# Modulation products of a two-block network: four blocks of k on the four column tiles of the array in one visit

## The chip, the cores and the metric

The kernel runs on one core of a Trainium2 chip. Times are microseconds (us) of device time of one execution; the time before is the median of three runs.

## The reference, cut to what matters

The network has a first block of two layers and a second block. Each layer of the first block scales and shifts its input and gates its output by vectors that are products of a condition vector with a large matrix, once for the latent rows (`c`) and once for the context rows (`c_ctx`):

```python
sc, scc = jax.nn.silu(c), jax.nn.silu(c_ctx)          # [1, 2048], [2048]
for l in range(DEPTH):                                 # two layers
    shift_l, scale_l, gate_l = jnp.split((sc @ mod_w[l] + mod_b[l])[:, None, :], 3, axis=-1)
    shift_c, scale_c, gate_c = jnp.split(scc @ mod_w[l] + mod_b[l], 3, axis=-1)
    hl = xl * (1.0 + scale_l) + shift_l                # 256 latent rows
    hc = xc * (1.0 + scale_c) + shift_c                # 256 context rows
    ...                                                # layer 0: a recurrence; layer 1: attention
    xl = layer_norm(DEEPNORM_ALPHA * xl + gate_l * yl, ln_g[l], ln_b[l])
    xc = layer_norm(DEEPNORM_ALPHA * xc + gate_c * yc, ln_g[l], ln_b[l])
```

`mod_w` is [2, 2048, 6144] in float32, 100 MB. Layer 0 is a mixer with a linear recurrence over 256 context and 256 latent tokens, in both directions, for 16 heads of 64; its input projection is 2048 x 6400. The second block has a cross attention to 256 memory rows, whose keys and values are products with `w_xkv`.

## The kernel before

The products with the modulation matrix have only two rows (`c` and `c_ctx`), so the condition is the stationary operand: for each block k of 128 rows of the matrix, `SC` holds a column pair, and a product takes 32 columns from there, of which the first two count. The moving operand is 128 x 512 elements of the matrix in float32. Thirty-two columns are one of four column tiles of the array, and the block k goes to tile `k % 4`, which writes partitions 32q to 32q + 31 of one accumulator; the four partial sums are added afterwards, by a product with `sel`. A column block of 512 outputs needs 16 blocks k.

`mod` (L332) is a generator that emits these products. It loads tiles of 128 x 2 x 512 (two blocks k, 512 KB) through SP's queue. Each step, a visit, takes one tile: two products on two column tiles (L354), tiles 0 and 1 or tiles 2 and 3. Eight visits make a column block; then ACT copies the accumulator (L359), and a ninth step turns or adds the partial sums (L364, L374). There are 24 column blocks in all: 8 of layer 0 in the head, the other 16 (layer 0's gate, all of layer 1) as fillers of layer 0's recurrence.

The order of PE is the order in which the Python code emits; a scheduler of the library orders DVE, SP and the other queues (and ACT after the first part of the head).

- The head (`head`, L1559): first the memory's rows are turned (L961) with one visit in each of eight steps; then the memory's keys (L1527 to L1529, weights split into a high part by ACT, L187, and a low part by DVE, L188) run with five visits to eight steps of six products, and with the filters (L1654, L1663) between. The tiles of `mod_w` go to a ring of eight buffers ("A"), seven loads ahead.
- The recurrence (`l0_body`, L802): 16 units, each cut into steps that wait on ACT and DVE (L685, L746, L751, L757, L763, L764). Between two steps `fill` emits products of `filler` for a number of us that follows from the work left and the steps left. `filler` yields groups of three products of the input projection (L468, L469, L470; 8 groups use up one weight chunk of 512 KB) and, of every 44 groups, takes a step of `mod` after each fourth until nine are done. `mod` yields an assumed 0.3 us for a visit and 0.9 us for the ninth step. Here the tiles of `mod_w` and the weight chunks share the buffers `raw`, four in all; `mod` loads one tile ahead.

Of the kernel before, what the change touches and what calls it, by code (L numbers as in the profile page):

```python
# [21 lines left out]
P = 128  # L22
# [27 lines left out]
def _consts():  # L50
    f = np.float32
    out = {}
# [40 lines left out]
    # real DFT of length 512, packed: rows 0..255 Re(0..255), row 256 Re(256), rows 257.. Im(1..255)  # L93
# [43 lines left out]
class _K:  # L137
# [12 lines left out]
    def big(s, tag):  # L150
        """sixteen [P, 2, 256] tiles (high and low part), in pairs"""
        out = _L()
        out.pairs = [s.T("%s%d" % (tag, j), [P, 2, 2, 256], F32R) for j in range(8)]
        out += [pr[:, i] for pr in out.pairs for i in range(2)]
        return out

    def big0(s, tag):
        """sixteen [P, 512] tiles, in pairs"""
        out = _L()
        out.pairs = [s.T("%s%d" % (tag, j), [P, 2, 512], F32R) for j in range(8)]  # L160
        out += [pr[:, i] for pr in out.pairs for i in range(2)]
        return out
# [5 lines left out]
    # ---------------------------------------------------------------- weights  # L168
# [32 lines left out]
    def formB(s, W, c0, toks, accs, nk=KT, sub=2):  # L201
        """toks: list of functions k -> (hi, lo) stationary APs"""
        nc = s.nc
        for kc in range(nk // sub):
            hi, lo = s.wload(W[kc * sub * P:(kc + 1) * sub * P, c0:c0 + 512].rearrange("(k p) c -> p k c", p=P), sub, 512)
            for kk in range(sub):
                k = kc * sub + kk
                for tk, acc in zip(toks, accs):
                    xh, xl = tk(k)
                    nc.tensor.matmul(acc, xh, hi[:, kk], start=k == 0, stop=False)  # L210
                    nc.tensor.matmul(acc, xh, lo[:, kk], start=False, stop=False)
                    nc.tensor.matmul(acc, xl, hi[:, kk], start=False, stop=k == nk - 1)
                yield

    # ---------------------------------------------------------------- setup
    def setup(s):
# [25 lines left out]
        # parameter vectors, feature-major  # L242
# [51 lines left out]
    def params(s, g):  # L294
        nc = s.nc
        ps = s.PS("sc")
        nc.tensor.transpose(ps[:, 0:128], s.prow[g], s.ident)
        nc.vector.tensor_copy(s.PT[:, g], ps[:, 0:128])
        if g != 1:
            return  # L300
        # 1 - mu, halves used by the tanh forms of the sigmoids
        s.PM = s.T("PM", [P, 128])
        nc.vector.tensor_scalar(s.PM, s.PT[:, 1], -1.0, 1.0, MUL, ADD)
        s.PH = s.T("PH", [P, 128])
        nc.vector.tensor_scalar(s.PH, s.PT[:, 1], 0.5, None, MUL)
        s.PHM = s.T("PHM", [P, 128])
        nc.vector.tensor_scalar(s.PHM, s.PT[:, 1], -0.5, 1.0, MUL, ADD)
# [7 lines left out]
    # ---------------------------------------------------------------- modulation  # L315
    def mod_prep(s):
# [8 lines left out]
        # column pairs (c, c_ctx) per k; each product takes 32 columns, of which the first two count  # L325
# [6 lines left out]
    def mod(s, l, j0, j1, ahead=1, ring=None):  # L332
        """columns of 512 of the modulation of layer l; yields the time of the products it has emitted"""
# [11 lines left out]
        for i, (j, kc) in enumerate(lst):  # L345
            for q in range(ahead + 1):
                load(i + q)
            raw = got.pop(i)
            if kc == 0:
                acc = s.PS("acc" if ring is None else "iv")  # L350
            for kk in range(2):
                k = kc * 2 + kk
                q = k % 4
                nc.tensor.matmul(acc[32 * q:32 * q + 32], s.SC[:, 2 * k:2 * k + 32], raw[:, kk], start=k < 4, stop=k >= 12, tile_position=(0, 32 * q))  # L354
            if kc < 7:
                yield 0.3
                continue
            rows = s.T("sg", [P, 512])
            nc.scalar.copy(rows, acc)  # L359
            yield 0.3  # L360
# [18 lines left out]
    # ---------------------------------------------------------------- layer 0  # L379
    def l0_rows(s):  # L380
        """token rows of the context and of x, as lists of 128-wide pieces"""
# [18 lines left out]
    def l0_h(s, toks):  # L400
        nc = s.nc
        s.AH, s.AL = s.big0("A"), s.big0("B")
        for k in range(16):
# [4 lines left out]
            md = s.MOD[0]  # lat: tokens 256:512, ctx: 0:256  # L408
# [21 lines left out]
    def l0_lora(s):  # L430
        nc, W = s.nc, s.I["ev_w_in"][0]
        # per direction: high part on the first 64 partitions, low part on the others
# [15 lines left out]
    def stream(s, srcs, ahead=1):  # L448
        """weight chunks (source, k, c) split ahead of their use: call with an index"""
# [12 lines left out]
    def atoms(s, i, hX, lX, acc):  # L462
        """formA as a generator that yields the time of the products it has emitted"""
# [38 lines left out]
    def cat_out(s, f, src, scale):  # L502
        """cat^T tile f = src * scale * silu(gate), to DRAM"""
# [55 lines left out]
    def wkv_prep(s, u):  # L559
# [4 lines left out]
        # shifted r, k, v  # L564
# [12 lines left out]
        # decay and in-context rate  # L577
# [9 lines left out]
        # normalised key  # L587
# [25 lines left out]
        # k'  # L613
# [6 lines left out]
        # bonus  # L620
# [20 lines left out]
    def wkv_half(s, u, g):  # L641
        """chunks 4g .. 4g + 3 of a unit: scaled operands, scores and the inverse"""
# [18 lines left out]
        # scores; AT = A^T - I  # L661
# [26 lines left out]
        # T = (I - A)^-1, block doubling in float16, then two refinements with float32 residuals  # L688
# [113 lines left out]
    def l0_body(s):  # L802
# [4 lines left out]
        # products that fill the waits of the recurrence  # L807
# [37 lines left out]
        def filler():  # L845
            side, n = (x for m in mods for x in m), 0
            for job in jobs:
                for c in job:
                    yield c
                    n += 1  # L850
                    if n % 44 % 4 == 0 and n % 44 < 9 * 4:
                        yield next(side, 0.0)
# [4 lines left out]
        left = [45 * 16 * 0.64 + 16 * 0.86 + 16 * (8 * 0.3 + 0.9)]  # L857
# [29 lines left out]
        def merge(a, b, side):  # L887
            """steps of a half's inverse and of a half's chain in turn, with the fillers between them"""
# [45 lines left out]
    # ---------------------------------------------------------------- helpers for token-major rows  # L934
# [19 lines left out]
    def toT(s, rows, dst, scale, bias, banks=("sc",)):  # L954
        """rows: two token tiles as four 512-wide pieces -> dst[k][:, 0/1, 256] = hi/lo of the transposed rows * scale + bias"""
# [26 lines left out]
    def split(s, dst, f, src):  # L982
        """src (float32, SBUF) -> hi/lo"""
# [3 lines left out]
    # ---------------------------------------------------------------- layer 0, output projection  # L987
    def l0_cat(s):
        """hi and lo of the concatenation, from DRAM; the last two tiles on the second call"""
# [17 lines left out]
    def l0_out_n(s, n, late=None):  # L1007
        """products of 512 output columns; yields the time of the products it has emitted"""
# [23 lines left out]
    def l0_out(s, pre, mem):  # L1032
        nc, I = s.nc, s.I
        # rows of alpha x + gate y: ctx tiles 0, 1 and lat tiles 2, 3
# [10 lines left out]
        for n in range(4):  # L1045
# [24 lines left out]
            if n == 2:  # L1070
                # h = (xn ln_g + ln_b) (1 + scale) + shift, in one scale and bias per feature
# [22 lines left out]
    # ---------------------------------------------------------------- layer 1  # L1094
# [16 lines left out]
    def rope(s, out, src, C, S, t):  # L1111
        """out = src * C + swap(src) * S for four heads of 128"""
# [21 lines left out]
    def gA(s, i, X, acc):  # L1134
        """formA on chunks i, i + 1 of the stream, in steps of two k"""
# [10 lines left out]
    def gB(s, i, toks, accs):  # L1146
        """formB on chunks i .. i + 7 of the stream, in steps of one k"""
# [12 lines left out]
    def weave(main, sides, first=0):  # L1160
        """steps of main with one step of each of the sides after each"""
# [11 lines left out]
    def l1_k(s, raws, Ck, Sk, kg, KTs):  # L1173
        """keys from their products: norm, rotation, transposition"""
# [74 lines left out]
    def l1(s):  # L1249
# [23 lines left out]
        # the last product of the memory's values fills the wait for the layer norm  # L1273
# [66 lines left out]
    def softmax(s, ps, n, scale):  # L1340
        """rows of softmax(scale * ps); scale a positive [P, 1] operand or number"""
# [13 lines left out]
    def proj_ln(s, idx, CAT, att, iM, iH):  # L1355
# [3 lines left out]
        # gain and bias of the layer norm times the gain of the next norm, per feature  # L1359
# [36 lines left out]
        # the first products of the next block's input projection, beside the rows' affine step and norm  # L1396
# [12 lines left out]
    def proj_add(s, W, CAT, nk=KT, g=None, ng=None):  # L1409
        """x += CAT W; with ng, the next norm's input as well: x times the gain, transposed piece by piece"""  # L1410
# [21 lines left out]
    # ---------------------------------------------------------------- second block  # L1432
    def sq_start(s):
        """sums of squares of the rows, piece by piece"""
# [16 lines left out]
    def rms_row(s):  # L1451
        """the rows' factors along the free dimension, on every partition"""
# [24 lines left out]
    def mem_rms(s):  # L1477
        """rows of the memory over their root mean square"""
# [35 lines left out]
    def mem_need(s):  # L1514
        """weight chunks of the memory's keys and of the first half of its values, in the order of their use"""
# [43 lines left out]
    def head(s):  # L1559
        """modulation of layer 0, keys and values of the memory and the filters side by side, then layer 0's input"""  # L1560
# [8 lines left out]
        mod = s.mod(0, 0, 8, ahead=7, ring=ring)  # L1569
        for i, _ in enumerate(s.mem_kv()):  # L1570
            next(mod)
# [5 lines left out]
        for _ in mem:  # L1577
# [4 lines left out]
            while m * 8 < i * 5:  # L1582
                m += 1
                next(mod, None)
# [15 lines left out]
    def sin(s, x, n):  # L1600
        """x <- sin(x), in place, x of shape [n, 256]"""
# [73 lines left out]
    def conv3(s, out, pad, name, f, nf):  # L1675
        """out = pad[t-1] w0 + pad[t] w1 + pad[t+1] w2; pad [P, 258]"""
# [10 lines left out]
    def group_rms(s, Y, gname, gi, f0):  # L1687
        """Y [P, 4, 256] feature-major; rms over the 512 features, gain, into the mix"""
# [118 lines left out]
    def gla(s):  # L1807
# [27 lines left out]
        # per direction: gates, scaled q and k, chunk states  # L1835
        PTm = s.T("S1", [P, 4, 2, 128])     # summed masked scores, [j, head, token tile, i]
# [3 lines left out]
        for d in range(2):  # L1840
            rv = (lambda a: a) if d == 0 else (lambda a: a[:, ::-1])
            for t in range(2):
# [38 lines left out]
                # scores  # L1881
# [11 lines left out]
                # states before each chunk  # L1893
# [42 lines left out]
    def cross(s):  # L1936
# [3 lines left out]
        for h in range(4):  # L1940
# [10 lines left out]
            for t in range(2):  # L1951
# [3 lines left out]
                if h + t == 0:  # L1955
                    # the rows' factors go with the scale of the scores
# [118 lines left out]
```

## Time and profile before

| what | us |
|---|---|
| median of three runs | 3797.99 |
| lowest and highest run | 3791.12, 3800.55 |
| span of the profiled execution | 3802.9 |
| head, about | 0 to 310 |
| layer 0's recurrence, about | 310 to 1560 |

The profile is of one execution; no other time than its span is given for it. In the profile a float32 product leaves two records, one of each pass, with a weight load for each. Rows of a timeline merge equal instructions that follow each other: their length goes from the first one's start to the last one's end, with a count. Ends of matmuls are modelled, so the distance between two starts tells more than a length.

### The profile page before, as it was taken

How to read it: one execution, taken by the hardware profiler on the slowest of the kernel's cores; microseconds unless marked ns; L12 is line 12 of the kernel's file. 1: busy time of each engine (PE TensorE's matmuls, PEld its weight loads, DVE VectorE, ACT ScalarE, POOL GpSimd, SP SyncE). 2: the span in 40 equal slices, each digit the busy share in tenths (PEclk: the TensorE clock that was granted, in tenths of full speed). 3: DMA queues.
4: the chain of work that ended last, by engine and by line, in shares of the span. 5: the costliest groups of instructions: out<-in, count | busy, mean ns of one | idle time of the engine just before them, and what ended most of it. 6: DMA issues, size and time to landing. Idle time of an engine off the chain costs nothing.

```text
span 3802.9 us, 64452 instructions
## 1 busy us (share of the span) xinstructions
PE 3713.1 (98%) x26401; PEld 2860.7 (75%) x26401; DVE 2182.7 (57%) x4007; ACT 1580.1 (42%) x2625; POOL 28.3 (1%) x56
## 2 busy tenths in 40 slices
PE   7999999999999999989999999999999999999998
PEld 4576566656666655657878888988989899999886
DVE  3244566666666666673475666765654555555544
ACT  3244433333433334442154654544454544444433
POOL 1000000000000000000000000000000000000000
PEclk9999999999999999989999999998999999999999
DMA  9985533333333434243344446743655566666654
GB/s 284 272 254 175 152 101 106 109 117 104 111 92 116 120 97 127 76 135 124 105 130 128 134 132 212 190 129 96 178 183 161 177 179 183 183 184 183 199 192 161
DMA packets 655682, 579.08 MB, mean 152 GB/s; under 512 B 24891, under 2 KB 498415, under 8 KB 655386
## 3 DMA queue, kind: packets, MB, share of 16 engines
q1 hardware_dynamic: 627008, 538.86, 47.5%
q10 hardware_dynamic: 24474, 29.09, 2.3%
q0 software_dynamic: 3904, 7.01, 0.7%
q8 instruction: 207, 3.39, 0.4%
q14 instruction: 89, 0.73, 0.1%
HBM read 547.32 MB, written 27.56 MB: 151 GB/s over the span
## 4 chain that ended last, share of the span: by engine, by line
issue 56%; PE 39%; DVE 2%; ACT 1%; DMA 1%; POOL 0%; ACTq 0%; SPq 0%; POOLq 0%; DVEq 0%
PE acc L468 7%; PE acc L469 4%; PE acc L470 4%; PE iv L685 4%; PE acc L354 3%; PE iv L354 2%; PE yb L764 2%; PE yb L763 1%; PE sc L670 1%; PE acc L1527 1%; PE acc L1529 1%; PE acc L1528 1%; PE yb L1663 1%; PE ch L746 1%; PE ch L757 1%
## 5 line engine op out<-in xcount | busy, mean ns | idle before, releaser
L188 DVE TENSOR_TENSOR wlo<-raw,whi 128x1024 fp32r<-128x1024 f32 (+1 forms) x857 | 928.6, 1087 | 817.8 <-ACT whi L187 788.7
L187 ACT CAST whi<-raw 128x1024 fp32r<-128x1024 f32 (+1 forms) x857 | 800.5, 939 | 1158.7 <-PE acc L198 278.4
L197 PE MATMUL acc<-A,whi 128*128 128x256 f32 (+1 forms) x1488 | 429.9, 289 | 0.8 <-ACT whi L187 0.8
L199 PE MATMUL acc<-A,wlo 128*128 128x256 f32 (+1 forms) x1488 | 429.9, 289 | 0.4 <-DVE wlo L188 0.4
L198 PE MATMUL acc<-A,whi 128*128 128x256 f32 x1456 | 416.5, 286 | 0.0
L468 PE MATMUL acc<-A,whi 128*128 128x512 f32 x768 | 370.1, 482 | 7.1 <-ACT ev L479 2.9
L469 PE MATMUL acc<-B,whi 128*128 128x512 f32 x768 | 304.2, 396 | 0.0
L470 PE MATMUL acc<-A,wlo 128*128 128x512 f32 x768 | 302.4, 394 | 0.0
L197 PEld LDWEIGHTS acc<-A,whi 128*128 128x128 f32 x1488 | 285.0, 192 | 5.4 <-ACT whi L187 1.3
L199 PEld LDWEIGHTS acc<-A,wlo 128*128 128x128 f32 x1488 | 285.1, 192 | 4.7 <-issue 0.8
L198 PEld LDWEIGHTS acc<-A,whi 128*128 128x128 f32 x1456 | 279.1, 192 | 2.2 <-issue 1.1
L468 PEld LDWEIGHTS acc<-A,whi 128*128 128x128 f32 x768 | 144.2, 188 | 133.9 <-issue 73.4
L199 PE MATMUL iv<-A,wlo 128*128 128x256 f32 x704 | 199.3, 283 | 0.2 <-DVE wlo L188 0.2
L197 PE MATMUL iv<-A,whi 128*128 128x256 f32 x704 | 199.2, 283 | 0.0
L198 PE MATMUL iv<-A,whi 128*128 128x256 f32 x704 | 199.2, 283 | 0.0
L470 PEld LDWEIGHTS acc<-A,wlo 128*128 128x128 f32 x768 | 145.4, 189 | 34.0
L469 PEld LDWEIGHTS acc<-B,whi 128*128 128x128 f32 x768 | 145.7, 190 | 21.3 <-issue 10.3
L354 PE MATMUL acc<-raw,SC 128*32 128x512 f32 x512 | 137.5, 616 | 0.0
L199 PEld LDWEIGHTS iv<-A,wlo 128*128 128x128 f32 x704 | 135.2, 192 | 0.4 <-DVE wlo L188 0.4
L197 PEld LDWEIGHTS iv<-A,whi 128*128 128x128 f32 x704 | 135.2, 192 | 0.0
L198 PEld LDWEIGHTS iv<-A,whi 128*128 128x128 f32 x704 | 135.2, 192 | 0.0
L714 DVE TENSOR_TENSOR t<-iv,t 128x256 f16<-128x256 f32 x128 | 54.2, 423 | 137.9 <-PE iv L685 137.4
(1555 smaller groups left out, 7453.8 us busy)
## 6 DMA issues: line engine op xcount, KB each, us to landing
raw<-w_gate_up SPq DMA_DIRECT2D x176, 512.0 KB
raw<-mod_w SPq DMA_DIRECT2D x128, 512.0 KB
raw<-ev_w_in SPq DMA_DIRECT2D x100, 512.0 KB
raw<-w_down SPq DMA_DIRECT2D x88, 512.0 KB
raw<-od_w_in SPq DMA_DIRECT2D x80, 512.0 KB
raw<-w_in SPq DMA_DIRECT2D x80, 512.0 KB
raw<-w_xkv SPq DMA_DIRECT2D x64, 512.0 KB
A<-mod_w SPq DMA_DIRECT2D x64, 512.0 KB
```

Source lines behind the costliest of these rows:

```text
L187: nc.scalar.copy(hi[:, q], raw[:, q])
L188: nc.vector.tensor_sub(lo[:, q], raw[:, q], hi[:, q].bitcast(F32))
L197: s.nc.tensor.matmul(acc, hi[:, k - k0], xh, start=k == 0, stop=False)
L198: s.nc.tensor.matmul(acc, hi[:, k - k0], xl, start=False, stop=False)
L199: s.nc.tensor.matmul(acc, lo[:, k - k0], xh, start=False, stop=k == n - 1)
L354: nc.tensor.matmul(acc[32 * q:32 * q + 32], s.SC[:, 2 * k:2 * k + 32], raw[:, kk], start=k < 4, stop=k >= 12, tile_position=(0, 32 * q))
L468: s.nc.tensor.matmul(acc, hi[:, k], hX[kx], start=kx == 0, stop=False)
L469: s.nc.tensor.matmul(acc, hi[:, k], lX[kx], start=False, stop=False)
L470: s.nc.tensor.matmul(acc, lo[:, k], hX[kx], start=False, stop=kx == 15)
L685: nc.tensor.matmul(ps[hs[h], c], l(hs[h], c), r(hs[h], c), start=True, stop=True)
L714: tt(T16 if l < 5 else T32, pt, T16, ADD)
L764: nc.tensor.matmul(o, ZV[:, h, c, :], STK[:, h, c, 1, :], start=False, stop=True)
```

## The change

A visit now takes two tiles of the matrix and emits four products, one on each column tile (L355). A column block has four visits instead of eight; with the step behind them it has five steps instead of nine. In the head `ahead` is gone: a visit asks for the loads up to seven tiles ahead of its first. In the recurrence the two tiles of the next visit are loaded right behind the present one. A visit yields 0.6 us instead of 0.3, `filler` takes a step after each ninth group, and the head's loops call `mod` half as often. The rest of the diff takes out comments and changes nothing (lines behind `mod` move down by 4 or 5).

```diff
-    def mod(s, l, j0, j1, ahead=1, ring=None):
+    def mod(s, l, j0, j1, ring=None):
...
-        for i, (j, kc) in enumerate(lst):
-            for q in range(ahead + 1):
+        for i in range(0, len(lst), 2):
+            j, kc = lst[i]
+            for q in range(2 if ring is None else 8):
                 load(i + q)
-            raw = got.pop(i)
             if kc == 0:
                 acc = s.PS("acc" if ring is None else "iv")
-            for kk in range(2):
-                k = kc * 2 + kk
-                q = k % 4
-                nc.tensor.matmul(acc[32 * q:32 * q + 32], s.SC[:, 2 * k:2 * k + 32], raw[:, kk], start=k < 4, stop=k >= 12, tile_position=(0, 32 * q))
-            if kc < 7:
-                yield 0.3
+            pair = [got.pop(i), got.pop(i + 1)]
+            for q in range(4):
+                k = kc * 2 + q
+                nc.tensor.matmul(acc[32 * q:32 * q + 32], s.SC[:, 2 * k:2 * k + 32], pair[q // 2][:, q % 2], start=k < 4, stop=k >= 12, tile_position=(0, 32 * q))
+            if ring is None:
+                load(i + 2)
+                load(i + 3)
+            if kc < 6:
+                yield 0.6
                 continue
...
-                    if n % 44 % 4 == 0 and n % 44 < 9 * 4:
+                    if n % 9 == 0:
                         yield next(side, 0.0)
...
-        left = [45 * 16 * 0.64 + 16 * 0.86 + 16 * (8 * 0.3 + 0.9)]
+        left = [45 * 16 * 0.64 + 16 * 0.86 + 16 * (4 * 0.6 + 0.9)]
...
-        mod = s.mod(0, 0, 8, ahead=7, ring=ring)
+        mod = s.mod(0, 0, 8, ring=ring)
         for i, _ in enumerate(s.mem_kv()):
-            next(mod)
+            if i % 2 == 0:
+                next(mod)
...
-            while m * 8 < i * 5:
+            while m * 16 < i * 5:
```

PE's order, at the start of the head (the memory's rows are turned from the tiles UV, BT; A_177 and so on are the ring's tiles). Before:

```order
L354 MATMUL iv<-A_177,SC 32x512 x2
L961 MATMUL iv<-k_65,UV_67 128x128
L961 MATMUL iv<-k_65,BT_75 128x128
L961 MATMUL iv<-k_65,UV_67 128x128
L961 MATMUL iv<-k_65,BT_75 128x128
L354 MATMUL iv<-A_178,SC 32x512 x2
```

and now:

```order
L355 MATMUL iv<-A_177,SC 32x512 x2
L355 MATMUL iv<-A_178,SC 32x512 x2
L965 MATMUL iv<-k_65,UV_67 128x128
L965 MATMUL iv<-k_65,BT_75 128x128
L965 MATMUL iv<-k_65,UV_67 128x128
L965 MATMUL iv<-k_65,BT_75 128x128
```

The second tile's two products moved up behind the first tile's, ahead of the turning of the next rows.

SP's order, in the first units of the recurrence (`raw<-ev_w_in` are weight chunks of the input projection, `raw<-mod_w` the modulation's tiles, the third kind reloads a product of the projection). Before:

```order
L171 DMA raw<-ev_w_in 128x8x128
L342 DMA raw<-mod_w 128x2x512
L171 DMA raw<-ev_w_in 128x8x128 x2
L342 DMA raw<-mod_w 128x2x512
L489 DMA r_4359<-rkv_0_2320 128x2x256
L342 DMA raw<-mod_w 128x2x512
L489 DMA k_4363<-rkv_1_2321 128x2x256
L171 DMA raw<-ev_w_in 128x8x128
```

and now:

```order
L171 DMA raw<-ev_w_in 128x8x128
L343 DMA raw<-mod_w 128x2x512 x2
L171 DMA raw<-ev_w_in 128x8x128 x2
L493 DMA r_4357<-rkv_0_2320 128x2x256
L343 DMA raw<-mod_w 128x2x512 x2
L171 DMA raw<-ev_w_in 128x8x128 x2
L493 DMA k_4361<-rkv_1_2321 128x2x256
L343 DMA raw<-mod_w 128x2x512 x2
L171 DMA raw<-ev_w_in 128x8x128
```

The modulation's loads stand in pairs now, with one or two chunks between two pairs.

## Rows read from the trace of the kernel before

**Rows 1.** The page's head: span, and each engine's busy us, share, instructions.

```profile
span 3802.9 us, 64452 instructions
...
PE 3713.1 (98%) x26401; PEld 2860.7 (75%) x26401; DVE 2182.7 (57%) x4007; ACT 1580.1 (42%) x2625; POOL 28.3 (1%) x56
```

**Rows 2.** Stretches: window and length, each engine's busy us, PEclk, DMA share, GB/s.

```profile
10.00:36.00 26.00, 18.48 (x90) 8.96 (x91) 15.66 (x37) 11.50 (x22) 4.34 (x9) 1.00 1.05 349
...
140.00:180.00 40.00, 40.00 (x207) 21.83 (x206) 9.96 (x12) 10.28 (x15) 1.08 (x2) 1.00 0.92 288
180.00:220.00 40.00, 40.00 (x204) 23.57 (x202) 7.20 (x10) 9.92 (x14) 0.00 (x0) 1.00 0.97 302
...
310.00:1560.00 1250.00, 1230.56 (x10864) 763.67 (x10864) 783.80 (x1875) 483.68 (x1059) 0.57 (x1) 0.99 0.39 115
```

**Rows 3.** PE's waits, 0:310, then 310:1560: total us, times, longest.

```profile
PE iv L364 <- ACT sg L359: 4.4, 1, 4.4
...
PE iv L354 <- DMA A<-mod_w: 1.6, 1, 1.6
...
PE ch L751 <- ACT R L748: 4.2, 10, 0.7
```

**Rows 4.** Stretches, line L354 alone: PE busy us (records), PEld busy us (records), clock.

```profile
0.00:310.00 310.00, 71.94 (x256) 9.49 (x256) 0.96 0.86 263
...
310.00:1560.00 1250.00, 137.52 (x512) 18.62 (x512) 0.99 0.39 115
```

**Rows 5.** Timeline of PE in the recurrence: start us, length us, instruction, count.

```profile
619.00 0.40 PE L470 MATMUL acc<-A,wlo 128*128 128x512 f32 x1
619.33 1.05 PE L354 MATMUL acc<-raw,SC 128*32 128x512 f32 x4
620.31 0.31 PE L685 MATMUL iv<-x,y 64*64 64x64 f16 x8
...
806.55 0.40 PE L470 MATMUL acc<-A,wlo 128*128 128x512 f32 x1
806.87 0.31 PE L685 MATMUL iv<-x,y 64*64 64x64 f16 x8
```

**Rows 6.** Timeline of PE in the head, the same columns.

```profile
19.49 1.92 PE L354 MATMUL iv<-A,SC 128*32 128x512 f32 x4 [1.57 <-DMA A<-mod_w]
...
122.67 0.28 PE L1527 MATMUL acc<-m,whi 128*128 128x256 f32 x1
...
122.90 0.28 PE L1529 MATMUL acc<-m,wlo 128*128 128x256 f32 x1
123.11 1.05 PE L354 MATMUL iv<-A,SC 128*32 128x512 f32 x4
124.09 0.39 PE L1527 MATMUL acc<-m,whi 128*128 128x256 f32 x1
124.32 0.28 PE L1528 MATMUL acc<-m,whi 128*128 128x256 f32 x1
...
128.32 1.96 PE L1663 MATMUL yb<-BK,S 128*128 128x512 f32 x4
130.12 1.88 PE L1663 MATMUL yb<-TW,S 128*128 128x512 f32 x4
```

**Rows 7.** PE's groups, 310:1560: count, then busy us, mean ns, idle before.

```profile
L468 PE MATMUL acc<-A,whi 128*128 128x512 f32 x704 | 339.3, 482 | 7.1 <-ACT ev L479 2.9 <-ACT pv L556 2.3 <-DVE pu L375 0.9
...
L354 PE MATMUL acc<-raw,SC 128*32 128x512 f32 x512 | 137.5, 616 | 0.0
```

**Rows 8.** Waits of SP's queue, 310:1560: total us, times, longest.

```profile
SPq L171 <- PE acc L354: 118.7, 22, 9.9
```

**Rows 9.** Timeline of DVE in the recurrence: the low part of a chunk's split.

```profile
628.16 1.29 DVE L188 TENSOR_TENSOR wlo<-raw,whi 128x512 fp32r<-128x512 f32 x2
```

**Rows 10.** DMA view of 0:250, then of 20:32 us.

```profile
DMA packets 62436, 69.54 MB, mean 278 GB/s; under 512 B 3547, under 2 KB 38796, under 8 KB 62422
...
DMA packets 2299, 4.48 MB, mean 373 GB/s; under 512 B 146, under 2 KB 146, under 8 KB 2299
```

More of the change, by code (lines that the diff above doesn't have):

```diff
@@ L359, in mod @@
             nc.scalar.copy(rows, acc)
-            yield 0.3
+            yield 0.6
             ps = s.PS("acc" if ring is None else "iv")
```

## The prediction

> **What bounds the kernel now.** I read the page first. PE is busy for 98% of a span of 3802.9 us, so time taken from PE's own stream shortens the run unless something else is close behind [rows 1]. The products that change run in two stretches only: the head (0 to 310 us), where modulation of layer 0 stands beside the memory's keys and the filters, and layer 0's recurrence (310 to 1560 us), where the rest fills waits. The second view is the time by stretch. In the recurrence PE is busy 1230.56 of 1250 us while DVE has 784, ACT 484 and the DMA engines are 0.39 busy; in the head PE is busy 40 of 40 us at full clock from 140 us on, but the DMA engines are at 0.92 to 0.97 there, and from 10 to 36 us, where PE has 18.5 of 26 us, they are full [rows 2]. The third is what PE waits for: in 1250 us of recurrence the largest entry is 4.2 us, and no entry there names a weight split or a load of mod_w; in the head one wait of 4.4 us (L364, on ACT) and one of 1.6 us on a load of mod_w concern the modulation [rows 3]. So the recurrence is bound by PE alone, the head by PE with DMA behind it.
>
> **What one visit costs.** L354 alone keeps PE busy for 71.94 us in the head and 137.52 us in the recurrence, with 256 and 512 records [rows 4]. A visit leaves four records (two products, each a float32 product of two passes), so that is 64 and 128 visits, 1.12 and 1.07 us each. The timeline says the same from outside. In the recurrence L470 is followed by L685 after 0.32 us (806.55 to 806.87); with a visit between them after 1.31 us (619.00 to 620.31): 0.99 us for the visit [rows 5]. In the head L1527, L1528 and L1529 follow each other at 0.12 us, two steps in 0.23 us (122.67 to 122.90); with a visit behind L1529 the next two steps take 122.90 to 124.32, 1.42 us: 1.19 us for the visit, with the change of tile shape into and out of it [rows 6]. The busy times lie between the two and I use them.
>
> The two column tiles of a visit already run side by side: its four records of 616 ns on average [rows 7], 2.46 us in sum, stand in a row of 1.05 us [rows 5]. A full-width float32 product of the same 512 columns (L1663) shows what a pass is: four passes go from 128.32 to 130.12, 0.45 us each [rows 6]. Two passes are 0.90 us, so the visit of 0.99 us is the time of one product and a change of shape; the second tile costs nothing that these rows resolve.
>
> **The change part by part.**
> *Half as many visits.* 32 go from the head and 64 from the recurrence: 71.94/2 + 137.52/2 = 36.0 + 68.8 = 104.7 us less on PE (from outside 64 x 0.99 = 63.4 to 64 x 1.19 = 76.2 for the recurrence, 38.1 for the head).
> *Two more tiles in each of the 96 that stay.* No row shows four column tiles at once. From below: nothing, since the second tile's cost cannot be seen; a gain is excluded, because the visit still needs two passes. From above: a whole second pair behind the first, two passes of 0.45 us, 0.90 us a visit and 86 us in all. I take 0.014 us a visit, 1.3 us in all: an estimate, two more starts at about the rounding of the timeline, from the case with two tiles, to which it is nearest.
> *Who hides what in the recurrence.* Removed visits also stood over waits of the recurrence. What mostly stands between two steps of the recurrence is one group of L468, L469, L470 alone: in the order of instructions 228 times before and 256 times now. Such spots have next to no waits today: all of PE's waits in this stretch are a few us an entry [rows 3]. I take 4 us of new waits for them and for the splits below.
> *Waits for a pair.* A visit now waits for two loads, and behind it in PE's queue stand the recurrence's products. In the recurrence both loads are issued just after the previous visit, nine groups earlier: 1250 us over 64 visits, some 19 us, on engines that are 0.39 busy. Nothing lost.
> *The SP queue.* The pair's two loads wait on SP for the visit that frees their buffers, and a weight chunk's load stands behind them. This is so today as well: SP's loads of weight chunks waited 118.7 us in total for L354, 22 times [rows 8], without a wait of PE [rows 3]. Of L468 there are 704 in 1250 us, 8 to a chunk, so 88 chunks of 14.2 us each [rows 7]; the longer half of a chunk's split takes 1.29 us [rows 9]. I leave it at the 4 us above.
> *The head and DMA.* From 0 to 250 us 69.54 MB move, at 278 GB/s; from 20 to 32 us, when almost all of it is loads of mod_w, the engines give 373 GB/s [rows 10]. PE would now want the same bytes in 250 - 36 = 214 us, 325 GB/s. That is under 373, so on average the loads keep up. In the first 40 us they don't: the share is full there [rows 2], and the 4.4 us of L364 [rows 3] stand at its end. Four of the 32 removed visits lie there, of eight, the first of which took 1.92 us [rows 6]: 4 x 1.1 to 4 x 1.9, some 6 us. They go but come back as a longer wait for the loads. With 1 us for the first visit, which waits for a second tile, I take 7 us off the head's 36.
>
> Sum: recurrence 68.8 - 0.9 - 4 = 63.9 us; head 36.0 - 0.4 - 7 = 28.6 us; together 92.5 us. Nothing behind the recurrence changes and PE bounds it too [rows 1]. The profiled execution goes from 3802.9 to 3710.4 us of span. It lies 4.9 us over the median of the runs (3797.99), so the median becomes 3705.5; I write **3705**.
>
> **A rule weighed.** In the visit two products overlap although each has two passes, so the second product's first pass does not wait for the first product's second [rows 5, 7]. The Trainium skill ("TensorE: Matmul & The Clock Gate", Part 3, "The mechanism") holds that matmuls start and end strictly in program order; whether four products' first passes all stand ahead of their second passes, no row here shows; if they don't, that rule leads to the first rival below. By the same part's span model (about 4 ns for each further tile) the 96 visits would take 96 x 2 x 4 ns = 0.8 us more, an estimate, in place of my 1.3 us.
>
> **The rivals.**
> *Products in pairs.* If the four are issued as two pairs, each with its two passes, and starts stay in order, the second pair's first pass begins with the first pair's second: three pass times instead of two, 0.45 us more a visit, 43 us. That leaves 104.7 - 43 - 5 of leaks = 57 us: 3741. For it: only pairs are seen together in any row. Against: nothing shows that the pairing is more than the code's own two products.
> *The second pair after the first.* Four moving tiles share a path that two fill: 0.90 us more a visit, 86 us, leaving 19 us: 3779. For it: two different tiles are the most that any row shows. Against: the second costs nothing, with no sign of a nearing limit.
> *The head gives nothing.* DMA is 0.92 to 0.97 busy from 140 to 220 us [rows 2]; were that the limit, PE would wait there for what it saved and only the recurrence's 64 us would stay: 3734. Against: PE has next to no wait for loads of mod_w today [rows 3], and 288 GB/s from 140 to 180 us [rows 2] is well under 373 [rows 10]. This case together with the one before gives about 3792, no change that a measurement of this kernel could tell (0.3%, 11 us).
> *Slower: weight chunks come late.* Two of the four raw buffers are held for the next pair over nine groups, and chunk loads queue on SP behind loads that wait for a visit. If the load and the split begin later than the chunk's 14.2 us allow, PE stops at every chunk. It decides from 92.5/88 = 1.05 us a chunk on; at 2 us a chunk it costs 176 us: 3798 - 92 + 176 = 3882. For it: SP's chunk loads already wait for L354, up to 9.9 us at a time [rows 8]. Against: not one wait of PE for a split in the recurrence today, and 14.2 us against a split of some 2.6 us and a load on DMA engines that are 0.39 busy [rows 2, 9].
>
> **How the numbers follow.** Forecast 0.66 (its own range 3688 to 3718: the outside prices without a leak give 3798 - 76.2 - 38.1 + 1.3 = 3685, twice the leaks 3717); head gives nothing 0.11; pairs 0.08; second pair after the first 0.05; no change 0.05; slower 0.05. The range 3688 to 3748 holds the first three, 0.85. Faster by over 0.3%: 0.66 + 0.11 + 0.08 + 0.05 = 0.90; within 0.3% 0.05; slower 0.05.
>
> **What would show it.** Right: visits with eight records, two passes long, a row of about 1.07 us, 32 in the head and 64 in the recurrence, some 105 us busy in all instead of 209; the products behind the recurrence starting some 92 us earlier, with about 29 of them gained by the head's end. Pairs: visits of some 1.4 us; no overlap: 1.9 us. DMA-bound head: PE waiting for A<-mod_w, several us in total. Late chunks: PE waiting for whi or wlo in the recurrence. Wrong altogether: equal visit lengths and a gain that is lost in waits for ACT or DVE, which would mean that the recurrence's own chain was close behind PE.

## The result and the profile after

The changed kernel takes 3736.96 us (median of four runs, 3724.09 to 3738.15) where the kernel before takes 3799.27: a ratio of 0.9832, with a 95% interval of 0.9816 to 0.9848. It is faster by 62 us by the medians, 64 by the ratio. The forecast was 92.5 us and 3705, with a range that reaches to 3748.

The page's head, which answers to [rows 1]: span, and busy time of the engines.

```profile
span 3734.0 us, 64397 instructions
...
PE 3615.6 (97%) x26401; PEld 2850.5 (76%) x26401; DVE 2181.9 (58%) x4007; ACT 1580.8 (42%) x2625; POOL 28.5 (1%) x56
```

PE is busy for 97.5 us less, yet the span is shorter by only 68.9 us, so PE stands idle for some 29 us more. Landmarks of the two traces say where. The first L468 (now L472) of the recurrence starts at 304.4 us instead of 330.2: the head gave 25.8 us. From the first to the last L468 the recurrence takes 1292.5 us instead of 1327.6: it gave 35.1 us. Behind that, where nothing was changed, the trace is shorter by 8.0 us; there PE has 55 us at half clock (1.2 GHz) instead of 72, and this figure lies anywhere from 55 to 85 us in the traces shown below, whose code is the same there. These 8 us are not the change's, and the medians, 62 us apart, don't show them. The landmarks themselves are good to 5 us or so either way: in the traces below that share a head's code its end lies from 325.7 to 330.2 us (the head of before) and from 296.0 to 305.2 (the changed one).

The visits are what was forecast. L355 (before: L354) alone, in the head and in the recurrence (window, its length, PE and PEld busy with their records, clock, DMA share, GB/s), answers to [rows 4]:

```profile
0.00:284.00 284.00, 38.18 (x256) 5.52 (x256) 0.95 0.90 286
304.00:1600.00 1296.00, 68.24 (x512) 10.14 (x512) 0.99 0.38 115
```

106.4 us in place of 209.5. A visit on the timeline, which answers to [rows 5], has eight records, and L689 (before: L685) follows 0.99 us after its start:

```profile
903.50 0.40 PE L474 MATMUL acc<-A,wlo 128*128 128x512 f32 x1
903.83 1.06 PE L355 MATMUL acc<-raw,SC 128*32 128x512 f32 x8
904.82 0.31 PE L689 MATMUL iv<-id,at 64*64 64x64 f16 x8
```

What PE waits for in the recurrence (total us, times, longest), against [rows 3]:

```profile
PE acc L472 <- ACT ev L483: 10.1, 9, 4.5
PE ch L755 <- ACT R L752: 8.2, 18, 1.1
PE ch L761 <- DVE UV L757: 6.4, 8, 1.7
PE acc L472 <- ACT pv L560: 4.2, 1, 4.2
PE acc L472 <- ACT pu L538: 3.4, 3, 1.3
PE acc L472 <- ACT ev L502: 3.3, 5, 0.9
```

Four of these six rows are one thing: L472, the first product of a group, waits for ACT to copy an accumulator out (L483, L502, L538, L560 are such copies). PE's groups there, against [rows 7]:

```profile
L472 PE MATMUL acc<-A,whi 128*128 128x512 f32 x768 | 370.6, 483 | 21.8 <-ACT ev L483 10.1 <-ACT pv L560 4.2 <-ACT pu L538 3.4
...
L355 PE MATMUL acc<-raw,SC 128*32 128x512 f32 x512 | 68.2, 605 | 0.0
```

The idle time ahead of L468 was 7.1 us [rows 7] and is 21.8 us.

**Where it stands in the program.** The input projection's work comes in 48 jobs of 16 groups; a job sums up in one accumulator, ACT copies it out, and the next job needs another one. There are two ("acc"), and a column block of the modulation keeps one of them from its first visit until its own copy. If it does so when a job ends, the next job can only take the accumulator that has just been filled, and waits for the copy. Before, a visit stood behind every fourth group, and 4 divides 16: at 24 of the 48 job ends a visit stood right in front of the next job's first group. Here is one in the trace of before, PE and ACT:

```profile
930.10 0.39 PE L470 MATMUL acc<-A,wlo 128*128 128x512 f32 x1
930.30 0.62 ACT L187 CAST whi<-raw 128x512 fp32r<-128x512 f32 x1
...
930.66 1.05 PE L354 MATMUL acc<-raw,SC 128*32 128x512 f32 x4
930.82 0.58 ACT L479 COPY ev<-acc 128x512 f32<-128x512 f32 x1
...
931.64 0.50 PE L468 MATMUL acc<-A,whi 128*128 128x512 f32 x1
```

The copy lies under the visit, and the next job starts without a wait. Now a visit stands behind every ninth group, which falls on a job's end only 3 times. The same job end after the change:

```profile
894.73 0.39 PE L474 MATMUL acc<-A,wlo 128*128 128x512 f32 x1
894.92 0.62 ACT L187 CAST whi<-raw 128x512 fp32r<-128x512 f32 x1
...
895.45 0.58 ACT L483 COPY ev<-acc 128x512 f32<-128x512 f32 x1
...
896.08 0.50 PE L472 MATMUL acc<-A,whi 128*128 128x512 f32 x1 [0.97 <-ACT ev L483]
...
896.97 0.31 PE L689 MATMUL iv<-y,x 64*64 64x64 bf16 x8
```

ACT has a weight cast ahead of the copy, as it had before, but no visit lies over the two, and PE stands idle for 0.97 us. For each of the 48 starts of a job I took the distance from the instruction ahead of it, less the median of that distance for the same pair of lines inside jobs. Before, the 48 have 8.4 us too much in sum; after, 25.4 us. After, 24.2 of them lie at the 26 ends at which the modulation holds an accumulator and no visit stands in front, and 1.2 us at the 19 at which it holds none.

### The profile page after: what moved, and what is told of

It reads as the page before. It is cut to its first block, busy times and chain, and to the rows that moved or that the text cites. A ratio compares the mean times of both kernels' runs of the same rounds, so it can differ in the third digit from the quotient of the medians.

```text
span 3734.0 us, 64397 instructions
## 1 busy us (share of the span) xinstructions
PE 3615.6 (97%) x26401; PEld 2850.5 (76%) x26401; DVE 2181.9 (58%) x4007; ACT 1580.8 (42%) x2625; POOL 28.5 (1%) x56
## 4 chain that ended last, share of the span: by engine, by line
issue 57%; PE 6%; DMA 0%; ACT 0%; DVE 0%; POOL 0%; POOLq 0%; DVEq 0%; ACTq 0%
PE acc L472 1%; PE acc L473 1%; PE acc L474 1%; PE iv L689 1%; DMA raw<-ev_w_in 0%; PE yb L768 0%; PE yb L767 0%; PE sc L674 0%; PE acc L355 0%; PE ch L761 0%; PE ch L750 0%; PE ch L755 0%; ACT ZV L715 0%; PE acc L557 0%; PE sc L633 0%
## 5 line engine op out<-in xcount | busy, mean ns | idle before, releaser
L472 PE MATMUL acc<-A,whi 128*128 128x512 f32 x768 | 370.6, 483 | 21.8 <-ACT ev L483 10.1
L472 PEld LDWEIGHTS acc<-A,whi 128*128 128x128 f32 x768 | 145.8, 190 | 102.6 <-issue 35.5
L701 DVE TENSOR_TENSOR x<-iv,k 128x256 f16<-128x256 f32 x160 | 67.7, 423 | 75.6 <-PE iv L689 73.7
```

The source lines that it names most:

```text
L472: s.nc.tensor.matmul(acc, hi[:, k], hX[kx], start=kx == 0, stop=False)
L701: tt(X16, px, b4(s.lv[d][l]), MUL)
```

## The experiments

Theory A says that these job ends are the loss: 17 of the recurrence's 29 us in excess starts. Theory B says that the recurrence's own chain (products that wait for ACT and DVE: L751, L757, L685, L670; now L755, L761, L689, L674) stands close behind PE, so that whatever is taken from the fillers comes back as waits there, and the job ends are only where it shows. Two more are named where they are tried: slower clock (C) and badly dealt fillers (D).

The table has all runs. "Below before" is one less the ratio, times 3798 us. The last four columns are from the trace: the recurrence from its first to its last L468, the idle time of PE ahead of L468 in it, the idle time ahead of all else, and the time at half clock. Each row has one trace, and the same code gives different ones: the recurrence of e3_head_only is that of before, and e4_rec_only has that of after; within these pairs its length differs by 5 us and its time at half clock by 10 to 14.

| kernel | ratio (95% interval) | below before | recurrence | idle, L468 | idle, others | half clock |
|---|---|---|---|---|---|---|
| before | 1 | 0 | 1327.6 | 7.1 | 14.9 | 23.9 |
| after | 0.9832 (0.9816 to 0.9848) | 64 | 1292.5 | 21.8 | 21.9 | 37.5 |
| e1_job_ends | 0.9833 (0.9818 to 0.9847) | 63 | 1286.1 | 7.0 | 30.4 | 37.5 |
| e2_before_shifted | 1.0059 (1.0044 to 1.0074) | -22 | 1348.7 | 21.1 | 19.0 | 20.5 |
| e3_head_only | 0.9931 (0.9915 to 0.9948) | 26 | 1323.0 | 8.0 | 13.9 | 13.7 |
| e4_rec_only | 0.9913 (0.9893 to 0.9932) | 33 | 1297.2 | 22.4 | 20.9 | 51.2 |
| e5_quarter_visits | 0.9702 (0.9682 to 0.9723) | 113 | 1242.4 | 3.4 | 38.5 | 41.0 |
| e6_credit_one | 0.9825 (0.9799 to 0.9851) | 66 | 1283.5 | 17.1 | 20.9 | 37.5 |
| e7_copies_first | 0.9846 (0.9829 to 0.9864) | 58 | 1293.1 | 15.9 | 24.2 | 47.8 |
| e8_copies_dve | 0.9948 (0.9933 to 0.9963) | 20 | 1338.4 | 38.3 | 26.2 | 99.0 |
| e9_one_job | 0.9805 (0.9790 to 0.9821) | 74 | 1282.9 | 0.4 | 31.7 | 34.1 |
| e10_one_job_credit | 0.9757 (0.9742 to 0.9771) | 92 | 1258.3 | 0.0 | 24.2 | 17.1 |
| e11_job_ends_credit | 0.9812 (0.9796 to 0.9829) | 71 | 1280.6 | 6.1 | 31.4 | 41.0 |
| e12_before_one_job | 0.9978 (0.9968 to 0.9989) | 8 | 1306.7 | 0.8 | 19.1 | 10.2 |

**The two halves apart.** Four-tile visits in the head alone, with the recurrence of before:

> Four-tile visits in the head alone, the recurrence as in the kernel before. By the landmarks of the two traces the head gave 25.8 us (forecast 28.6): about 3773. If part of the head's gain is only passed on by chance to the recurrence's start (weights loaded late, DMA), it is smaller: 3780 or more.

and in the recurrence alone, with the head of before:

> Four-tile visits in the recurrence alone, the head as in the kernel before. By the landmarks the recurrence gave 35 us where 63.9 were forecast: about 3764. If the loss in the recurrence came from the head's earlier end (the two halves do not add), the recurrence alone gives more: 3735 to 3750.

26 and 33 us, 59 in sum, against 64 for both. They add, within the intervals, and both are near what the landmarks say. The head is as forecast; what is missing is missing in the recurrence.

**Taking the cover away without the change.** The kernel before with its two-tile visits moved by two groups:

```diff
-                    if n % 44 % 4 == 0 and n % 44 < 9 * 4:
+                    if n % 44 % 4 == 2 and n % 44 < 9 * 4:
```

> The kernel before, with its two-tile visits moved by two groups, so that none stands right in front of a job's first group; as many visits of the same size, as many groups. Theory A: the cover at 24 job ends is gone, 8 to 17 us more than before, 3807 to 3816. Theories B and C: visits are where they were in number and in the chain, so no change, 3795 to 3803.

22 us slower. PE's group in its trace:

```profile
L468 PE MATMUL acc<-A,whi 128*128 128x512 f32 x768 | 370.8, 483 | 21.1 <-ACT ev L479 10.2 <-ACT ev L498 4.8 <-ACT pu L534 3.2
```

That is more than the 8 to 17 us that A had expected. The idle time is that of the changed kernel, 21.1 us, with no change to the number or size of visits, and less time at half clock than before. That speaks for A and against C: the alignment alone was worth some 20 us to the kernel before.

**Putting the cover back.** The changed kernel with its visits at each job's 8th and 16th group:

```diff
             for job in jobs:
+                n = 0
                 for c in job:
...
-                    if n % 9 == 0:
+                    if n % 8 == 0:
```

> The changed kernel, but the fillers count their groups afresh for each job of 16 groups, and a visit follows each 8th group: one of every two visits then stands right in front of the next job's first L472, the one that waits for ACT to copy the accumulator out. Theory A (part of the lost 29 us are job ends that no visit covers any more; the excess wait at 48 job ends rose from 8.1 to 25.2 us): about 15 us less than the changed kernel, 3720 to 3725. Theory B (the recurrence's own chain and the pacing of the fillers took it, job ends are a sign only): no change, 3734 to 3740. Theory C (a slower clock in waits): no change in the waits' sum, a time within 5 us of the changed kernel.

No change that the runs can tell (63 against 64 us, each within 6), against A's 3720 to 3725. The idle time of L472 is back at 7.0 us, but that of all else has risen by 8.5 us. Half of that, 4.3 us, is this row:

```profile
PE ch L755 <- ACT R L752: 12.5, 24, 1.1
```

Another part is a wait of 3.3 us of L557, a product of other fillers that needs an accumulator too. So there is something in B as well. I read it so: a visit covers one wait; moved to a job's end, it is missing where it covered a wait of the chain. That 128 visits were enough for both and 64 are not was not tried by itself.

**Making ACT faster at the job ends.** The copies of the projection's accumulators set ahead in ACT's order, then done by DVE:

```diff
-            nc.scalar.copy(o, acc)
+            with s.prio(100):
+                nc.scalar.copy(o, acc)
```

> The changed kernel with the copies of the input projection's accumulators set ahead in ACT's order (the scheduler's priority of the recurrence's inverse). Theory A: the waits of L472 for ACT (21 us) shrink to under 10 and most of it is gained, 3720 to 3728. Theory B: those waits shrink and come back on the recurrence's chain, which ACT now serves later, 3732 to 3745.

```diff
-            nc.scalar.copy(o, acc)
+            nc.vector.tensor_copy(o, acc)
```

> The changed kernel with the same copies done by DVE instead of ACT. Theory A: DVE has fewer waits of its own, the waits of L472 shrink, 3720 to 3730. Theory B: the recurrence's chain runs over DVE as well, so they come back as waits of L674, L761, L689 for DVE, 3732 to 3750.

The first took 6 us from L472's idle time and gave 2 to the others, with no gain in time. The second made it worse by 44 us. In its trace half of the 40 copies start sooner than on ACT (0.04 us behind the job's last product, against 0.34), but some come late: 13 end over 1.5 us behind that product, against 5 on ACT, and the mean start is at 0.86 us, against 0.42. L472 stands idle for 38.3 us, 30.1 of it for DVE, and 99 us of the recurrence run at half clock. Neither takes away what makes PE wait, the single accumulator.

**Fewer visits, and the accumulator free.** One visit in four stays in the recurrence, so that the modulation holds its accumulator for one group only; this kernel leaves three quarters of the recurrence's modulation products out.

> The changed kernel with one visit in four in the recurrence: 16 in place of 64 (only the last four of sixteen blocks of k are multiplied, so the modulation that the recurrence computes is incomplete), with their loads, and the fillers' time spread accordingly. 48 visits of 1.0 us leave PE. Theory A (job ends that lost their cover because the modulation holds one of the two accumulators): the bank is now held for one group only, the waits of L472 for ACT go, and all 48 us and some 15 more are gained: 3675 to 3690. Theory B (the recurrence's own chain stands close behind PE, so work taken from the fillers is worth ever less): 10 to 28 us, 3709 to 3727, and the waits on the chain (L755, L761, L689) grow by about what is missing.

3683 us, 49 (by the ratios) to 54 less than the changed kernel, for 48 visits of 1.0 us each. That lies in A's range, but without most of the 15 us more that A had added. The reason is only half A's. The idle time of L472 goes down by 18.4 us, as A says, and that of all else up by 16.6, as B says:

```profile
PE ch L755 <- ACT R L752: 12.1, 23, 1.1
PE sc L674 <- DVE BK L639: 6.5, 7, 1.7
PE ch L761 <- DVE UV L757: 5.5, 9, 1.0
PE ch L750 <- DVE ZV L764: 3.3, 1, 3.3
```

**The accumulator free with all visits kept.** A column block's four visits now lie inside one job, behind its 3rd, 6th, 9th and 12th group, in 16 of the 48 jobs, so that the modulation holds nothing when a job ends:

```diff
+                    if n % 16 == 0 and c < 0.8:
+                        owed += 16
+                        on = owed >= 45
+                        owed -= 45 * on
                     yield c
                     n += 1
-                    if n % 9 == 0:
+                    if q % 5 == 4 and n % 16 == 2 or on and n % 16 in (3, 6, 9, 12) and q % 5 < 4:
                         yield next(side, 0.0)
+                        q += 1
```

> The changed kernel with a column block's four visits inside one job of the input projection (behind its 3rd, 6th, 9th and 12th group, in 16 of the 48 jobs, the turning behind the 2nd group of the next job), so that the modulation holds an accumulator at no job's end. The work is the same, the waits of L472 should fall from 22 to under 6 us in any case. Theory A (they are a loss of their own): 15 to 20 us less than the changed kernel, 3715 to 3722. Theory B (what is taken from them comes back on the recurrence's chain, which has its waits where no visit stands now): 0 to 8 us less, 3729 to 3737. A third way: the loads of 1 MB each three groups (2.6 us) are too many, PE waits for raw<-mod_w, and it is slower than the changed kernel, 3745 and more.

The median is 3721.56, 15 us under the changed kernel: at A's end. By the ratios it is 10, between A's 15 to 20 and B's 0 to 8, and the intervals overlap a little. In the trace the waits of L472 are gone, and a new one is small:

```profile
L472 PE MATMUL acc<-A,whi 128*128 128x512 f32 x768 | 370.5, 482 | 0.4 <-ACT pv L560 0.4
...
L355 PE MATMUL acc<-raw,SC 128*32 128x512 f32 x512 | 73.9, 605 | 2.9 <-DMA raw<-mod_w 2.9
```

Of the 21.4 us, 9.8 came back as other idle time.

**The dealing of the fillers.** `fill` hands out time between the recurrence's steps, and a visit that takes 1.0 us counts as 0.6. Counted as 1.0, alone, with the visits of e1, and with those of e9:

```diff
-                yield 0.6
+                yield 1.0
...
-        left = [45 * 16 * 0.64 + 16 * 0.86 + 16 * (4 * 0.6 + 0.9)]
+        left = [45 * 16 * 0.64 + 16 * 0.86 + 16 * (4 * 1.0 + 0.9)]
```

> The changed kernel with a visit counted as 1.0 us instead of 0.6 by the code that deals the fillers out; the total it reckons with is changed with it. The work is the same. Theory D (the fillers are dealt out badly, a visit counts too little): 8 us or more less than the changed kernel, 3715 to 3729. Theories A and B: the same sum of waits in other places, 3732 to 3742.

> The kernel of e1_job_ends (a visit in front of each held job end) with a visit counted as 1.0 us. e1_job_ends had the waits of L472 down to 7 us, and 8 of the 15 us came back on the chain (L755, L689). If the dealing is what put them there, 8 to 15 us less than e1_job_ends, 3720 to 3727; if not, 3730 to 3738.

> The kernel of e9_one_job with a visit counted as 1.0 us by the code that deals the fillers out, as in e6_credit_one (which gave 8 us less than the changed kernel, within its interval). If the two add: e9_one_job less 5 to 9 us, so 3706 to 3715 by theory A and 3720 to 3731 by theory B.

Alone it gives nothing that can be told (66 against 64 us), with the visits at the job ends 8 us more than those alone (the intervals overlap). With the accumulator free it gives 18 us more than e9_one_job, more than the 5 to 9 expected: 3705.82 us, 92 us below before, and faster than both kernels (its interval and that of the changed kernel lie apart). Against e6_credit_one, which counts a visit as it does and keeps the visits of the changed kernel, it is 26 us less, with intervals apart: this pair says most clearly that it pays to hold no accumulator at a job's end. PE's group, and waits of the recurrence's chain:

```profile
L472 PE MATMUL acc<-A,whi 128*128 128x512 f32 x768 | 365.9, 476 | 0.0
...
PE ch L755 <- ACT R L752: 7.6, 17, 1.0
PE ch L761 <- DVE UV L757: 7.0, 8, 1.5
...
PE sc L674 <- DVE BK L639: 3.4, 4, 1.0
```

Against e9_one_job the idle time ahead of all else is lower by 7.5 us and half clock by 17 us, which at half speed is 8.5 us of work. How the dealing brings that about was not followed step by step.

**Are the two edits a gain of their own?** Both on the kernel before, whose eight visits then stand inside one job:

> The kernel before with both edits of e10_one_job_credit: a column block's eight visits (two tiles each) stand inside one job of the input projection, a visit counts as 1.0 us. It says whether those edits are worth as much without the four-tile visits. If they only mend what the change broke: within 8 us of the kernel before, 3790 to 3803 (the waits of L468, 7 us before, go), and four tiles in one visit are then worth 85 to 95 us by themselves. If they are a gain of their own that has nothing to do with the change: 20 to 32 us less than before, 3766 to 3778, and four tiles are worth 60 to 72.

8 us (4 to 12), far nearer to "they only mend" than to the other. Its one trace has a recurrence shorter by 21 us, 7 of them by less time at half clock; the runs decide. Of the 28 us between the changed kernel and e10_one_job_credit some 20 are thus, by difference, what the change had broken, and four tiles in one visit are worth 84 us (0.9978 less 0.9757) where both kernels are laid out for it.

## Why the prediction was right, and where it was wrong

*Half as many visits.* Right: 104.7 us of busy time forecast, 209.5 - 106.4 = 103.0 measured.

*Two more tiles.* Right: 0.014 us a visit forecast, 0.013 measured (the next instruction starts 996 ns after a visit's first start, before 983). That the term was next to nothing was argued; that it fits to 0.001 us is luck, since it was put at the rounding of the timeline. The starts inside a visit lie at 0, 7, 13, 20 and 453, 460, 467, 473 ns: all four first passes, then all four second ones. So the rivals of pairs and of a second pair behind the first fall. By the span model of the Trainium skill ("TensorE: Matmul & The Clock Gate", Part 3), some 4 ns for each further tile, the two would have cost 8 ns; the trace has 13, and the measurement decides.

*The head.* Right in its sum: 28.6 us forecast, 25.8 by the landmarks, 26 (20 to 32) in e3_head_only. L355's busy time fell by 33.8 us, so 8 leaked where I had 7.4. The first two visits take 3.10 and 1.56 us, the first of them behind late loads. The wait that I saw come back in the first 45 us went from 4.4 to 5.9 us only, and now L1531 has it, for ACT; ACT's weight cast ahead of that had waited 6.67 us for a load of w_xkv, not of mod_w. New are 6.0 us of waits of L1659 (before: L1654, 0.3 us), 4.0 of them for a load of the filters. So the leak has its size in part by luck. These are the answers to [rows 2]:

```profile
140.00:180.00 40.00, 37.94 (x216) 25.02 (x215) 9.07 (x10) 12.19 (x18) 1.09 (x2) 0.91 0.93 299
180.00:220.00 40.00, 40.00 (x283) 28.62 (x282) 10.88 (x13) 11.51 (x16) 0.00 (x0) 1.00 1.03 338
```

DMA gives 338 GB/s and PE is busy all the same; its only wait for the modulation's loads is this one, so the rival of a head that gives nothing falls too:

```profile
PE iv L355 <- DMA A<-mod_w: 1.7, 1, 1.7
```

*Late weight chunks.* Right: SP's loads of chunks wait for L355 as they did for L354 [rows 8], and no wait of PE for a split stands among the large ones:

```profile
SPq L171 <- PE acc L355: 123.7, 28, 16.4
```

*Who hides what in the recurrence.* This is the step that failed. I wrote that removed visits "also stood over waits" and took 4 us for it. The recurrence gave 35.1 us by the landmarks (33 in e4_rec_only) where 63.9 had been forecast. In these two traces PE's idle time there grew by 21.8 us, and 13.6 us more at half clock make 6.8 us: 28.6 us in place of the 4.

The other 4 us that are missing are the price of a visit, a term that was too large. L355's own busy time in the recurrence is 69.3 us less, but that of PE as a whole only 56.9 (1305.6 us from 330.19 to 1657.79 before, 1248.8 from 304.39 to 1596.91 after), or 63.7 without the slower clock, since the row of a visit, 1.05 us, reaches over the start of the next instruction at 0.98. By that distance, which the forecast had too and set aside, 64 visits are 62.9 us and not 68.8.

The 4 us were sized by PE's waits as they were, "a few us an entry", and those are the waits that the visits left over. What they covered is in no wait row. It had to be read from PE's order: at 24 of 48 job ends a visit stood in front of the product that needs the accumulator, every fourth group fits 16 and every ninth doesn't. Of the 21.8 us of idle time 14.7 stand ahead of L472 (17 with all that is too much in starts of jobs), and freeing the accumulator gave 10 to 15 us back. Waits of L751, L757 and L685 grew by 3.3, 5.3 and 2.0 us, that of L553 by 1.0; L670 and L629 lost 4.5 us of theirs. Only the job ends were taken apart by runs. What share the waits have in the longer time at half clock stays open.

The measured 3737 us lies in the stated range only because that was drawn to hold two rivals as well, "head gives nothing" at 3734 and "products in pairs" at 3741. It is nearer to both than to 3705, and the forecast's own range of 3688 to 3718 missed it. The traces show neither rival, so the time alone would have pointed to a wrong cause.

The forecast had named this case as "wrong altogether": equal visits and a gain lost in waits for ACT or DVE, "which would mean that the recurrence's own chain was close behind PE". The waits came, but the conclusion was half wrong. Most of them were for a copy outside the chain, and with the accumulator free and the visits counted right the recurrence gives 69.3 us in the trace (1327.6 to 1258.3) and some 66 by the runs (92 less the head's 26), where 63.9 had been forecast. That this kernel's 3705.82 us is the forecast's 3705 is chance: some 8 of its 92 us could have been had before the change (e12_before_one_job), which leaves 84 for the visits, 58 of them in the recurrence. The chain is close as well: that is part of why e1_job_ends gained nothing and 17 us came back in e5_quarter_visits.

The Trainium skill ("Perfetto Trace Analysis", "Optimizing Tensor Performance", "Matmuls") says that independent groups of matmuls should rotate through PSUM banks, so that the copy of one lies beside the matmuls of the next. The trace agrees: 1.2 us at 19 job ends with two banks to turn between, 24.2 at 26 with one. The Trainium skill ("TensorEngine Tiling (Array Packing)", "PSUM Bottleneck") has it that after a speedup by tiles the copies may come to bound, and advises both ScalarE and VectorE for them. No run here deals the copies out to both; all 40 of the projection's own copies moved from ACT to DVE cost 44 us (e8_copies_dve).

## What to carry to other kernels

Work that fills waits gives back less than its own length when it is taken out, and the wait rows don't say how much less, because they show only what it leaves uncovered: before removing or moving a filler, look in the engine's order at what stands right behind it and ask what that would wait for. When a period changes (4 to 9), check it against every other period on the engine, here the 16 groups of a job. And where a long-lived sum holds one of two accumulators, keep it inside one use of the other: here freeing it took the wait away, while covering it again mostly moved it.

## What the runs showed of the hardware that was not expected

Four float32 products on four column tiles take 996 ns to the start of the next instruction, two on two tiles 983, and the first passes of all four (starts at 0 to 20 ns) stand ahead of the second ones (453 to 473 ns).

A single long wait was also followed by a slower clock. One behind a copy, and what comes after it (PE's timeline in the changed kernel):

```profile
744.87 1.02 PE L603 MATMUL sc<-tb,k 128*128 128x512 f32 x2
750.12 0.79 PE L472 MATMUL acc<-A,whi 128*128 128x512 f32 x1 [4.23 <-ACT pv L560]
750.71 0.63 PE L473 MATMUL acc<-B,whi 128*128 128x512 f32 x1
751.13 0.63 PE L474 MATMUL acc<-A,wlo 128*128 128x512 f32 x1
751.69 0.42 PE L689 MATMUL iv<-t,at 64*64 64x64 f16 x8
```

and the windows from 745.5 to 750 and from there to 760:

```profile
745.50:750.00 4.50, 0.39 (x1) 0.00 (x0) 1.07 (x2) 4.46 (x8) 0.00 (x0) 0.93 0.67 204
750.00:760.00 10.00, 9.88 (x61) 6.50 (x62) 6.60 (x15) 2.37 (x6) 0.00 (x0) 0.52 0.09 28
```

PE is idle for 4.23 us, and the next 10 us run at a granted clock of 0.52, which is 1.2 GHz for nearly all of them. A group of three products takes 1.57 us there (750.12 to 751.69), against 0.89 us in the stretch shown above (896.08 to 896.97 in the same trace). Ten us at half speed are some 5 us lost on top of the wait, an estimate. It is no fixed price: the other wait of over 4 us in the recurrence, 4.50 us up to 366.46, was followed by only some 3.4 us at half clock (0.51 from 367.0 to 370.5).
